# The values' raw compression weights loaded with the second key block into a pool of their own, their last block after the prompt's attention scratch, and the prompt mLSTM denominators on VectorE alone

## The chip, the cores and the metric

The kernel runs on one core of a Trainium2 chip. Its time is the device time of one execution in microseconds (us). Engines are named as in the profile: PE is TensorE (PEld its weight load, PEq its sequencer), DVE VectorE, ACT ScalarE, POOL GpSimd, SP SyncE, which here does nothing but issue DMAs.

## What is computed

The reference is one decoder layer of a hybrid model: a prompt of 512 tokens and a decode step for eight sample rows go through attention over paged caches (compressed blocks, selected blocks and a window) beside an mLSTM, then a projection, cross attention and an MLP. Two pieces of it matter here. The first compresses cached keys and values: 16 rows of the cache make a chunk, and two neighbouring chunks go through a two-layer perceptron.

```
def compress(kv, pe, w1, b1, w2):
    ch = kv.reshape(b, nc, CMP_STRIDE, hk, dh).transpose(0, 1, 3, 2, 4).reshape(b, nc, hk, half)
    first = ch @ w1[:half]
    second = ch @ w1[half:]
    second = jnp.concatenate([second[:, 1:], jnp.zeros_like(second[:, :1])], axis=1)
    hid = first + second + (pe.reshape(-1) @ w1 + b1)
    return jax.nn.gelu(hid) @ w2
k_cmp = compress(kc_all, *w['cmp_k'])
v_cmp = compress(vc_all, *w['cmp_v'])
```

`w1` has 2048 x 256 entries, 2 MB for the keys and 2 MB for the values. The second piece is the denominator of the mLSTM:

```
den = jnp.sum(a, axis=2) + w_inter * jnp.einsum('bhd,blhd->blh', n, qi)
h_out = num / jnp.maximum(jnp.abs(den), jnp.exp(-m_q))[..., None]
```

## The kernel before, in words

The stage runs from about 235 to 440 us. It is written as Python generators that are woven together: in the background `compress(0)` (keys) and then `compress(1)` (values), in the foreground a chain of `front()` (the prompt's mLSTM, with the prompt's attention over compressed blocks, `cmp_prompt`, in between), `mlstm_s` (the mLSTM of the sample rows) and `sample` (their attention). A scheduler then sets each engine's order; every engine takes its own instructions strictly in that order, and pools of buffers decide what may be in flight. Engines that are ready have no way past an instruction that waits.

`compress` walks over 8 blocks b of cached rows and 4 parts t of the 2048 rows of `w1`. For each t, `load_w1` (L583 to L588) fetches the raw weights by four DMAs of 128 KB, and `weights` splits them: a high half `w1h` by ScalarE (L213), the low half `w1l` = raw minus high by VectorE (L214), and GpSimd adds two raw halves to `ws` (L1134). TensorE then multiplies three times (L218 high x high, L219 low x high, L220 high x low) and once with the sum (L1296). `xf`, `xh`, `xl`, `xs` are the gathered rows, turned and split in the same manner; `cgat` is where gathers (POOL, L573) put them.

The raw weights of the values lie in three places. `wr` holds t = 0 and 1 (eight DMAs, 1 MB). `vcn` holds t = 2. `po` (`po2` in the code) and `r` (`r3`) hold the halves of t = 3. The key weights went through `vcn`, `po` and `r` too, so these are used twice. In the kernel before, `wr` is a tile of the pool `w1r`, which is opened, together with `pp` (the prompt columns of the values, L1167 and L1168), only when the prompt's mLSTM is done; all four parts are loaded there, with the two `vcn` halves as their previous readers allow and `po` as early as its last key reader permits.

`cmp_prompt` handles four tiles i of 128 prompt tokens. Each has a scratch `csb` (128 x 256): scores plus mask by VectorE (L1369), minimum (L1371, L1372), difference by POOL (L1373), exponential by ScalarE, sum and reciprocal on VectorE (L1376 to L1378), gates (L1379), product by POOL (L1380); TensorE transposes it (L1387) and ScalarE puts it into `PcT` (L1388). `csb` has two buffers in a pool. `cmp_consts` uses one of them earlier as `cd`.

The prompt's mLSTM projects with `wqk` (L781, one buffer, loaded for the next head after the present one's last use, L802) by L799 and L802, and closes each tile with `dn`: an absolute value by ScalarE (L835), maximum (L836) and reciprocal (L837) by VectorE, and a scaling by ScalarE (L838). `mlstm_s` follows with L948 to L1120: transpositions L991, scores L1006 and `As` (L1009 to L1012), `n0T` (L1035 on TensorE, L1036 on VectorE), state transpositions L1058 into `CT`, and L1065, the product with the old state, which needs them. `nxt<-cur` (L1305, L1306) are small DMAs of the compression.

Of the kernel before, what the change touches and what calls it, by code (L numbers as in the profile page):

```python
# [6 lines left out]
F32 = mybir.dt.float32  # L7
# [4 lines left out]
OP = mybir.AluOpType  # L12
# [24 lines left out]
def body(tc, I, O, stage=99, dbg=None):  # L37
    nc = tc.nc
    with ExitStack() as top:
# [37 lines left out]
        def push(name, **kw):  # L77
            st = ExitStack()
            right[name] = st
            return pool(name, stack=st, **kw)  # L80

        def pop(name):
            right.pop(name).close()
# [682 lines left out]
        def mlstm():  # L766
# [62 lines left out]
            def value(h, i):  # L829
# [4 lines left out]
                dn = ml.tile([128, 1], F32, name="dn", bufs=4)  # L834
                nc.scalar.activation(dn, pn[:, 128:129], AF.Abs)  # L835
                nc.vector.tensor_tensor(dn, dn, eN[:, i, h:h + 1], op=OP.max)  # L836
                nc.vector.reciprocal(dn, dn)  # L837
# [98 lines left out]
        def cmp_consts(pk_):  # L936
            CB = pk_.tile([128, 4, 8, 32], F32, name="CB")
            cd = pk_.tile([128, 8, 32], F32, name="csb", bufs=2)[:, 0:4]
            nc.gpsimd.iota(cd, pattern=[[128, 4], [-16, 32]], base=-31, channel_multiplier=1,
# [181 lines left out]
        def compress(kv):  # L1121
# [49 lines left out]
            def produce(b, t):  # L1171
# [9 lines left out]
                if b == 0 and t > 0:  # L1181
                    weights(t, raws[t])
                if kv == 0 and b > 0 and "w" not in cgs and "ml" not in right and "mlstm" in done:
                    wp_ = push("w1r", side="left")
                    cgs["w"] = wp_.tile([128, 2, 2, 2, 256], F32, name="wr")
                    prompt_cols(1, r3, wp_.tile([128, 512], F32, name="pp"))
                    for u in range(4):
                        load_w1(1, u, [cgs["w"][:, u, s] for s in range(2)] if u < 2 else
                                ([vr[:, s] for s in range(2)], pr_)[u - 2])
                xf = cw.tile([128, 4, 128], F32, name="xf", bufs=2)  # L1190
# [14 lines left out]
                if b == 0 and t == 3:  # L1205
                    if kv == 1:
                        pop("w1r")
                    done.add(("w", kv))
# [136 lines left out]
        def cmp_prompt():  # L1345
# [17 lines left out]
            for i in range(5):  # L1363
                if i < 4:
                    sb = pk_.tile([128, 8, 32], F32, name="csb", bufs=2)
                    S = bank(psp)
# [467 lines left out]
        def front():  # L1834
            cb = cgs["cb"] = cmp_prompt()
            n = 0
            for x in mlstm():
                yield x
                n += 1
                if ("p", 0) in done and n % 2 == 0:  # L1840
                    next(cb, None)

        fg = chain(paced(front(), 1.3), paced(mlstm_s(), 2), paced(sample(), .8), open_late())
        flip[1] = 4
# [772 lines left out]
```

## Time and profile before

| | us |
|---|---|
| median of 3 runs | 1234.26 |
| lowest and highest of the 3 | 1231.63, 1235.07 |
| the profiled execution's own time | 1243.24 |
| its span (first to last instruction) | 1241.5 |
| TensorE busy in the span | 1174.3 (95%) |
| VectorE, ScalarE, GpSimd busy | 841.2, 612.4, 558.6 |
| mean granted TensorE clock | 0.974 |

Rows of the profile give a start and a duration in us, the engine, the line, output and input by the names of the program, and in brackets how long the engine had been idle and what ended that. Busy times of windows and the granted clock (1.00 is 2.4 GHz, 0.50 is 1.2 GHz) are read side by side: an engine that is nearly always busy in a window bounds it, and TensorE that is busy at half clock is slow without being idle.

### The profile page before, as it was taken

Reading aid. Unit: us, or ns where it says so; the run is one execution under the profiler, and the core shown is the slowest. Engines: PE = TensorE matmul, PEld = TensorE weight load, DVE = VectorE, ACT = ScalarE, POOL = GpSimd, SP = SyncE. Lnnn points to the kernel's source line nnn. Section 1 sums busy time; section 2 is a strip of 40 time slices with the busy share of each in tenths; the row PEclk is TensorE's granted clock in tenths of the full one; section 3 lists DMA queues with packets and bytes.
Section 4 is the critical chain, followed back from the end, with each engine's and each line's share of the span. In section 5 each row is a group of like instructions: output and inputs, shape, how many; then the busy total and the mean of one; then the engine's idle time right before and its main releaser. Section 6 shows DMA issues by size and latency. Waiting matters only on the chain.

```text
span 1241.5 us, 24581 instructions
## 1 busy us (share of the span) xinstructions
PE 1174.3 (95%) x9220; PEld 1066.7 (86%) x9220; DVE 841.2 (68%) x1901; ACT 612.4 (49%) x1414; POOL 558.6 (45%) x686
## 2 busy tenths in 40 slices
PE   7999999899997989988999989999899999999996
PEld 5998999588885878854999987599899999999996
DVE  6337683567787687653754756554998888888874
ACT  5235665745545444466542423342665565555452
POOL 1013353566666266542342100043885576476342
PEclk9999999899997999999999998999999999999998
DMA  7324240141253185566767298630032333322411
GB/s 232 102 53 105 86 153 1 51 137 44 78 171 115 42 283 176 178 227 205 206 135 171 83 239 288 231 128 2 1 119 86 103 96 107 106 94 77 137 52 73
DMA packets 141769, 154.30 MB, mean 124 GB/s; under 512 B 17449, under 2 KB 123689, under 8 KB 141394
## 3 DMA queue, kind: packets, MB, share of 16 engines
q1 hardware_dynamic: 131922, 119.17, 32.0%
q0 software_dynamic: 9728, 33.56, 8.3%
q8 instruction: 73, 1.20, 0.4%
q14 instruction: 46, 0.38, 0.1%
HBM read 141.67 MB, written 13.12 MB: 125 GB/s over the span
## 4 chain that ended last, share of the span: by engine, by line
PE 49%; DVE 8%; ACT 3%; DMA 2%; issue 2%; SPq 1%; POOL 1%; POOLq 0%; DVEq 0%; ACTq 0%
PE xc L2291 7%; PE xa L2291 7%; PE bd L2291 5%; PE tp L2291 5%; PE bd L220 3%; PE bd L219 3%; PE bd L218 3%; DVE sp L2231 1%; DMA mkv<-in_cache_mem_k 1%; PE xa L1296 1%; PE tp L1518 1%; PE bd L2190 1%; PE xa L218 1%; PE xa L219 1%; PE xa L220 1%
## 5 line engine op out<-in xcount | busy, mean ns | idle before, releaser
L214 POOL TENSOR_TENSOR al<-fraw,ah 128x512 fp32r<-128x512 f32 (+1 forms) x104 | 127.5, 1227 | 152.4 <-ACT ah L213 124.0
L213 ACT ACTIVATE whi<-wraw 128x1024 fp32r<-128x1024 f32 (+3 forms) x74 | 62.5, 890 | 57.5 <-DMA wraw<-in_w_xv 28.2
L214 DVE TENSOR_TENSOR wlo<-wraw,whi 128x1024 fp32r<-128x1024 f32 (+3 forms) x74 | 73.6, 1026 | 19.1 <-ACT whi L213 19.0
L213 ACT ACTIVATE ah<-fraw 128x512 fp32r<-128x512 f32 (+1 forms) x112 | 65.8, 593 | 38.0 <-PE xc L2291 11.8
L218 PE MATMUL bd<-w1h,xh 128*128 128x256 f32 x256 | 82.6, 325 | 0.9 <-issue 0.9
L220 PE MATMUL bd<-w1h,xl 128*128 128x256 f32 x256 | 75.6, 298 | 3.0 <-DVE xl L214 3.0
L1198 POOL TENSOR_TENSOR xs<-xf 128x256 f32<-128x256 f32 x64 | 55.8, 878 | 50.2 <-PE xa L1296 30.5
L219 PE MATMUL bd<-w1l,xh 128*128 128x256 f32 x256 | 75.7, 297 | 0.0
L1296 PE MATMUL xa<-ws,xs 128*128 128x256 f32 x256 | 71.2, 400 | 2.4 <-DVE bq L1470 1.3
L625 POOL TENSOR_SCALAR sb<-sb,rs,gat 128x128 f32<-128x128 f32 (+3 forms) x64 | 46.1, 724 | 54.4 <-DVE rs L624 40.2
L213 ACT ACTIVATE xh<-xf 128x512 fp32r<-128x512 f32 x64 | 40.0, 629 | 45.5 <-DVE xf L1191 20.0
L213 ACT ACTIVATE ah<-sp 128x512 fp32r<-128x512 f32 (+1 forms) x64 | 35.5, 555 | 50.1 <-DVE sp L2231 22.8
L220 PEld LDWEIGHTS bd<-w1h,xl 128*128 128x128 f32 x256 | 48.9, 192 | 6.4 <-DVE xl L214 3.8
L1296 PEld LDWEIGHTS xa<-ws,xs 128*128 128x128 f32 x256 | 46.5, 201 | 8.5 <-issue 2.9
L218 PEld LDWEIGHTS bd<-w1h,xh 128*128 128x128 f32 x256 | 49.1, 193 | 5.0 <-issue 3.9
L214 DVE TENSOR_TENSOR xl<-xf,xh 128x512 fp32r<-128x512 f32 x64 | 47.5, 746 | 8.6 <-ACT xh L213 7.7
L219 PEld LDWEIGHTS bd<-w1l,xh 128*128 128x128 f32 x256 | 49.4, 193 | 4.5 <-issue 2.8
L219 PE MATMUL bd<-hlo,whi 128*128 128x272 f32 x176 | 52.0, 296 | 0.0
L218 PE MATMUL bd<-hhi,whi 128*128 128x272 f32 x176 | 51.7, 294 | 0.0
L1191 DVE STREAM_TRANSPOSE xf<-cgat 128x512 f32<-128x512 f32 x64 | 44.7, 703 | 10.2 <-POOL xs L1198 8.4
L220 PE MATMUL bd<-hhi,wlo 128*128 128x272 f32 x176 | 51.3, 292 | 0.0
L2231 DVE TENSOR_TENSOR sp<-fraw 128x512 f32<-128x512 f32 (+1 forms) x32 | 47.8, 1494 | 0.2
(990 smaller groups left out, 4667.9 us busy)
## 6 DMA issues: line engine op xcount, KB each, us to landing
fraw<-in_w_gate SPq DMA_DIRECT2D x11, 1024.0 KB
fraw<-in_w_up SPq DMA_DIRECT2D x11, 1024.0 KB
fraw<-in_w_down SPq DMA_DIRECT2D x24, 384.0 KB
mkv<-in_cache_mem_k SPq DMA_DIRECT2D x64, 128.0 KB
mkv<-in_cache_mem_v SPq DMA_DIRECT2D x16, 512.0 KB
wraw<-in_w_in SPq DMA_DIRECT2D x8, 512.0 KB
wraw<-in_w_xq SPq DMA_DIRECT2D x4, 1024.0 KB
wraw<-in_w_xk SPq DMA_DIRECT2D x4, 1024.0 KB
```

The source lines that it names most:

```text
L213: nc.scalar.activation(hi, src, AF.Copy)
L214: (eng or nc.gpsimd).tensor_tensor(lo, src, hi, op=OP.subtract)
L218: nc.tensor.matmul(out, ah, bh, start=first, stop=False, **kw)
L219: nc.tensor.matmul(out, ah, bl, start=False, stop=False, **kw)
L220: nc.tensor.matmul(out, al, bh, start=False, stop=last, **kw)
L625: (nc.vector, nc.gpsimd)[1].tensor_scalar(sb[:, :n], sb[:, :n], rs, gat[:, i, 3 * h + 1 + br:3 * h + 2 + br], op0=OP.mult, op1=OP.mult)
L1191: nc.vector.transpose(xf.rearrange("p a (q i) -> p q a i", q=4), gs[0].rearrange("p (q t a i) -> p t q a i", q=4, t=4, a=4)[:, t])
L1198: nc.gpsimd.tensor_tensor(xs_.rearrange("p c (v j) -> p v c j", v=2), xg[:, 0], xg[:, 1], op=OP.add)
L1296: nc.tensor.matmul(dst[2], ops[2][:, kk], w1s[t][2][:, kk], start=t == 0 and kk == 0, stop=t == 3 and kk == 1, skip_group_check=True)
L1518: nc.tensor.transpose(p[:, 128 * i:128 * i + 128], srcs(i), ident)
L2231: nc.vector.tensor_tensor(o, a, b, op=op)
L2291: nc.tensor.matmul(p[:, :HALF], w[a][:, k], x[b_][:, k], start=first and k == 0 and i == 0, stop=last and k == n - 1 and i == 2, skip_grou ...
```

## The change

Three edits go together. First, the pool `w1r` with the tile `wr` is opened before the foreground chain is made, and the weights of the values for t = 0 and 1 are loaded when block b = 1 of the keys is produced, one part with t = 0 and one with t = 1; after the mLSTM a second pool `w1p` holds only `pp`, and only t = 2 and 3 are loaded there. Second, to make room, the scratch of `cmp_prompt` is no longer a tile of its own: `csb` uses the two halves of `po2` by turns, and `cd` uses the first of them. Third, the denominators: VectorE computes max(-den, e) straight from PSUM, then the maximum with den, so that ScalarE's absolute is gone.

```diff
--- before.py
+++ after.py
@@ -832,8 +832,9 @@
                     nc.tensor.matmul(pn[:, :129], st["A", h, k][:, 128 * (i - k):128 * (i - k) + 128], vmn[:, k, h],
                                      start=k == 0, stop=k == i)
                 dn = ml.tile([128, 1], F32, name="dn", bufs=4)
-                nc.scalar.activation(dn, pn[:, 128:129], AF.Abs)
-                nc.vector.tensor_tensor(dn, dn, eN[:, i, h:h + 1], op=OP.max)
+                e = eN[:, i, h:h + 1]
+                nc.vector.scalar_tensor_tensor(dn, pn[:, 128:129], -1.0, e, op0=OP.mult, op1=OP.max)
+                nc.vector.tensor_tensor(dn, dn, pn[:, 128:129], op=OP.max)
                 nc.vector.reciprocal(dn, dn)
                 nc.scalar.activation(hN[:, h, i], pn[:, :128], AF.Copy, scale=dn)
                 jk = ml.tile([128, 128], B16, name="jk")
@@ -935,7 +936,7 @@
 
         def cmp_consts(pk_):
             CB = pk_.tile([128, 4, 8, 32], F32, name="CB")
-            cd = pk_.tile([128, 8, 32], F32, name="csb", bufs=2)[:, 0:4]
+            cd = po2[:, 0:128].rearrange("p (i s) -> p i s", i=4)
             nc.gpsimd.iota(cd, pattern=[[128, 4], [-16, 32]], base=-31, channel_multiplier=1,
                            allow_small_or_imprecise_dtypes=True)
             for h in range(8):
@@ -1180,13 +1181,14 @@
                         gather_cmp(*nxt, q)
                 if b == 0 and t > 0:
                     weights(t, raws[t])
+                if kv == 0 and b == 1 and t < 2:
+                    load_w1(1, t, [cgs["wv"][:, t, s] for s in range(2)])
                 if kv == 0 and b > 0 and "w" not in cgs and "ml" not in right and "mlstm" in done:
-                    wp_ = push("w1r", side="left")
-                    cgs["w"] = wp_.tile([128, 2, 2, 2, 256], F32, name="wr")
+                    wp_ = push("w1p", side="left")
+                    cgs["w"] = cgs.pop("wv")
                     prompt_cols(1, r3, wp_.tile([128, 512], F32, name="pp"))
-                    for u in range(4):
-                        load_w1(1, u, [cgs["w"][:, u, s] for s in range(2)] if u < 2 else
-                                ([vr[:, s] for s in range(2)], pr_)[u - 2])
+                    for u in (2, 3):
+                        load_w1(1, u, ([vr[:, s] for s in range(2)], pr_)[u - 2])
                 xf = cw.tile([128, 4, 128], F32, name="xf", bufs=2)
                 nc.vector.transpose(xf.rearrange("p a (q i) -> p q a i", q=4),
                                     gs[0].rearrange("p (q t a i) -> p t q a i", q=4, t=4, a=4)[:, t])
@@ -1204,6 +1206,7 @@
                     st["e", t] = hi, lo
                 if b == 0 and t == 3:
                     if kv == 1:
+                        pop("w1p")
                         pop("w1r")
                     done.add(("w", kv))
                 st[b, t] = [(xh[:, :, g], xl[:, :, g]) for g in range(2)] + [xs_]
@@ -1362,7 +1365,7 @@
             yield
             for i in range(5):
                 if i < 4:
-                    sb = pk_.tile([128, 8, 32], F32, name="csb", bufs=2)
+                    sb = po2[:, 256 * (i % 2):256 * (i % 2) + 256].rearrange("p (h s) -> p h s", h=8)
                     S = bank(psp)
                     for v in range(2):
                         nc.tensor.transpose(S[:, 128 * v:128 * v + 128], ST[:, v, 128 * i:128 * i + 128], ident)
@@ -1840,6 +1843,7 @@
                 if ("p", 0) in done and n % 2 == 0:
                     next(cb, None)
 
+        cgs["wv"] = push("w1r", side="left").tile([128, 2, 2, 2, 256], F32, name="wr")
         fg = chain(paced(front(), 1.3), paced(mlstm_s(), 2), paced(sample(), .8), open_late())
         flip[1] = 4
         burst(fg, 8)
```

SyncE's order near the middle of `compress(0)`, after the prompt columns `xf<-cd` of the keys. `wqk` are the projection weights of head 2, `po_3201` and `r_3207` the buffers of t = 3. Before:

```order
L1156 DMA hidt<-in_cmp_pe_k 4x256
L1157 DMA hidt<-in_cmp_b_k 4x32
L1167 DMA xf<-cd_81 128x1x512
L588 DMA po_3201<-in_cmp_w_v 128x1x256 x2
L1167 DMA r_3207<-cd_82 128x1x512
L781 DMA wqk<-in_w_qm 128x128
L781 DMA wqk<-in_w_km 128x128
L756 DMA out<-kcT 24x512
L757 DMA out<-kcT 3x512
L1305 DMA nxt<-cur 112x256
```

After:

```order
L1157 DMA hidt<-in_cmp_pe_k 4x256
L1158 DMA hidt<-in_cmp_b_k 4x32
L1168 DMA xf<-cd_81 128x1x512
L588 DMA wr<-in_cmp_w_v 128x1x256 x8
L781 DMA wqk<-in_w_qm 128x128
L781 DMA wqk<-in_w_km 128x128
L1168 DMA r_3207<-cd_82 128x1x512
L756 DMA out<-kcT 24x512
L757 DMA out<-kcT 3x512
L1308 DMA nxt<-cur 112x256
```

The eight `wr` loads have come in ahead of `wqk`, the two `po` loads have gone, and the prompt columns into `r` stand behind `wqk`.

SyncE's order where the mLSTM of the prompt ends. Before:

```order
L954 DMA n_4539<-in_state_n 32x128
L956 DMA n_4541<-in_state_n 8x512
L1305 DMA nxt<-cur 112x256
L1306 DMA nxt<-cur 15x256
L1305 DMA nxt<-cur 112x256
L1306 DMA nxt<-cur 15x256
L588 DMA wr<-in_cmp_w_v 128x1x256 x8
L588 DMA r_3207<-in_cmp_w_v 128x1x256 x2
L1091 DMA out<-nsn 8x512
L1156 DMA hidt<-in_cmp_pe_v 4x256
```

After:

```order
L955 DMA n_4546<-in_state_n 32x128
L957 DMA n_4548<-in_state_n 8x512
L588 DMA po_3201<-in_cmp_w_v 128x1x256
L1308 DMA nxt<-cur 112x256
L1309 DMA nxt<-cur 15x256
L588 DMA po_3201<-in_cmp_w_v 128x1x256
L588 DMA r_3207<-in_cmp_w_v 128x1x256 x2
L1150 DMA w_5307<-in_cmp_w_v 128x2x64
L1157 DMA hidt<-in_cmp_pe_v 4x256
```

Ten loads of the values' weights before, four after, and two of these (`po`) are loads that stood at the early place.

VectorE's order right behind `wc`, a small vector of the samples' mLSTM (about 369 us in the trace before). `w1l_...` are the low halves of the values' weights. Before:

```order
L973 TENSOR_TENSOR wc<-m_99,smS 4x8
L214 TENSOR_TENSOR xl<-xf,xh 128x2x4x64
L1332 TENSOR_TENSOR ys<-xa,cur 128x256
L1234 SCALAR_TENSOR_TENSOR hid<-hidt,hid 128x512
L1372 TENSOR_SCALAR cmn<-cmn 128x8
L962 TENSOR_SCALAR nsl<-sel 4x128
L982 COPY msk<-bm 32x32
L1000 COPY bm_4623<-bm 32x8 x3
L1191 STREAM_TRANSPOSE xf<-cgat 128x4x4x32
L214 TENSOR_TENSOR xl<-xf,xh 128x2x4x64
L1333 TENSOR_TENSOR ys<-ys,bd 128x256
```

After:

```order
L974 TENSOR_TENSOR wc<-m_99,smS 4x8
L1336 TENSOR_TENSOR ys<-ys,bd 128x256
L1337 TENSOR_TENSOR ys<-bd,nxt 128x256
L214 TENSOR_TENSOR w1l_5302<-wr,w1h_5301 128x1024
L214 TENSOR_TENSOR xl<-xf,xh 128x2x4x64
L963 TENSOR_SCALAR nsl<-sel 4x128
L214 TENSOR_TENSOR xl<-xf,xh 128x2x4x64
L1375 TENSOR_SCALAR cmn<-cmn 128x8
L214 TENSOR_TENSOR w1l_5340<-wr,w1h_5339 128x1024
L208 COPY kcT<-xc 128x127
L1193 STREAM_TRANSPOSE xf<-cgat 128x4x4x32
L214 TENSOR_TENSOR w1l_5361<-vcn,w1h_5360 128x1024
```

Three splits of the values' weights stand here now; before, that of `vcn` stood 26 rows behind `wc` and the two of `wr` some 20 rows behind that.

## Rows read from the trace of the kernel before

**Rows 1.** The head of the page: span, and each engine's busy time, share and instructions.

```profile
span 1241.5 us, 24581 instructions
PE 1174.3 (95%) x9220; PEld 1066.7 (86%) x9220; DVE 841.2 (68%) x1901; ACT 612.4 (49%) x1414; POOL 558.6 (45%) x686
```

**Rows 2.** Windows of the stage: start and end, length, then busy us (and instructions) of PE, PEld, DVE, ACT and POOL, the granted clock, the share of the DMA engines that is busy, and GB/s.

```profile
262.00:360.00 98.00, 96.86 (x700) 85.30 (x699) 70.59 (x170) 50.79 (x149) 63.51 (x76) 1.00 0.28 85
360.00:378.00 18.00, 16.02 (x108) 13.93 (x107) 15.03 (x41) 7.35 (x18) 12.03 (x19) 0.91 0.65 194
378.00:392.00 14.00, 8.38 (x66) 6.16 (x64) 12.87 (x24) 9.94 (x20) 12.76 (x12) 0.72 0.42 130
392.00:412.00 20.00, 17.32 (x101) 14.32 (x101) 11.16 (x22) 10.57 (x26) 5.41 (x7) 0.68 0.15 51
```

**Rows 3.** The timeline of TensorE in the hole: start, duration, engine, line, operation.

```profile
381.04 0.44 PE L1387 MATMUL tp<-ident,csb 128*128 128x128 f32 x2
...
383.70 0.44 PE L1006 MATMUL tp<-qsT,ksT 128*32 128x32 f32 x8 [1.79 <-ACT PcT L1388]
...
387.68 1.91 PE L1016 MATMUL tp<-wi,sel 4*128 4x32 f32 x8 [2.94 <-DVE As L1012]
...
391.44 0.58 PE L218 MATMUL bd<-w1h,xh 128*128 128x256 f32 x1 [0.85 <-issue]
...
398.14 0.24 PE L1035 MATMUL tp<-ident,n 32*128 32x32 f32 x1
...
402.62 1.11 PE L1216 MATMUL xc<-ident,ys 128*128 128x128 f32 x4 [2.67 <-ACT kcT L206]
...
408.90 0.43 PE L1065 MATMUL po<-CT,Qz 128*32 128x129 f32 x8
```

**Rows 4.** The timeline of ScalarE: the splits that waited for a raw weight.

```profile
390.33 1.06 ACT L213 ACTIVATE w1h<-wr 128x1024 fp32r<-128x1024 f32 x1 [2.98 <-DMA wr<-in_cmp_w_v]
...
399.29 1.06 ACT L213 ACTIVATE w1h<-wr 128x1024 fp32r<-128x1024 f32 x1 [3.23 <-DMA wr<-in_cmp_w_v]
401.76 0.63 ACT L213 ACTIVATE w1h<-r 128x512 fp32r<-128x512 f32 x1 [1.42 <-DMA r<-in_cmp_w_v]
```

**Rows 5.** The timeline of VectorE: the low halves of weights, of a key weight (246.25) and of the values' weights, and `n0T`.

```profile
246.25 1.21 DVE L214 TENSOR_TENSOR w1l<-vcn,w1h 128x1024 fp32r<-128x1024 f32 x1
...
379.26 2.83 DVE L214 TENSOR_TENSOR w1l<-vcn,w1h 128x1024 fp32r<-128x1024 f32 x1
...
391.42 2.07 DVE L214 TENSOR_TENSOR w1l<-wr,w1h 128x1024 fp32r<-128x1024 f32 x1 [0.54 <-issue]
...
400.38 1.33 DVE L214 TENSOR_TENSOR w1l<-wr,w1h 128x1024 fp32r<-128x1024 f32 x1 [6.13 <-ACT w1h L213]
402.43 1.21 DVE L214 TENSOR_TENSOR w1l<-r,w1h 128x512 fp32r<-128x512 f32 x1 [0.71 <-ACT w1h L213]
403.56 0.18 DVE L1036 COPY n0T<-tp 128x32 f32<-128x32 f32 x1
```

**Rows 6.** The timeline of SyncE: when a DMA, or a run of equal ones, was issued, and how long the issuing took with its waits in between.

```profile
245.07 0.54 SPq L1167 DMA_DIRECT2D xf<-cd  x1
248.13 1.12 SPq L588 DMA_DIRECT2D po<-in_cmp_w_v  x2
251.27 0.52 SPq L1167 DMA_DIRECT2D r<-cd  x1
251.89 0.41 SPq L781 DMA_DIRECT2D wqk<-in_w_qm  x1
...
381.06 7.02 SPq L588 DMA_DIRECT2D wr<-in_cmp_w_v  x8
388.18 5.90 SPq L588 DMA_DIRECT2D r<-in_cmp_w_v  x2
```

**Rows 7.** Windows of the two half-clock stretches in the hole, columns as in group 2.

```profile
401.30:408.10 6.80, 5.49 (x23) 4.83 (x24) 5.46 (x11) 3.60 (x8) 2.41 (x2) 0.50 0.01 3
384.20:397.90 13.70, 9.90 (x47) 7.83 (x48) 9.42 (x21) 8.80 (x23) 7.20 (x8) 0.50 0.46 146
```

**Rows 8.** DMA traffic of SyncE's queue: packets, MB and the share of the 16 engines' time, first from 216 to 230 us (key weights, no gathers), then from 247 to 252.2 and from 388 to 394 (both beside gathers).

```profile
q1 hardware_dynamic: 1081, 0.92, 19.9%
...
q1 hardware_dynamic: 286, 0.39, 21.1%
...
q1 hardware_dynamic: 320, 0.32, 18.4%
```

**Rows 9.** The timeline of POOL beside the 2.83 us split.

```profile
379.68 1.27 POOL L1134 TENSOR_TENSOR ws<-vcn 128x512 f32<-128x512 f32 x1
380.93 1.74 POOL L1198 TENSOR_TENSOR xs<-xf 128x256 f32<-128x256 f32 x1
```

**Rows 10.** The tile `dn`: least, median and greatest duration in ns, first and last start; below, the idle time of L838's engine before it, with its count.

```profile
L835 ACT ACTIVATE dn<-tp x16: 149/160/179, 258.1 to 321.7; 128x1 f32<-128x1 f32 x16
L836 DVE TENSOR_TENSOR dn<-dn,eN x16: 118/151/768, 259.4 to 322.4; 128x1 f32<-128x1 f32 x16
...
  DVE dn L837: 14.0, 9
```

**Rows 11.** The timeline of TensorE: the last use of the `wqk` of head 1, and the first of head 2.

```profile
251.36 0.30 PE L802 MATMUL tp<-xc,wqk 128*128 128x32 f32 x2
...
262.30 1.02 PE L799 MATMUL tp<-xc,wqk 128*128 128x512 f32 x2
```

## The prediction

> **What bounds the kernel now.** I read the head of the page first: TensorE is busy 1174.3 of 1241.5 us, VectorE 841.2 [rows 1]. An average of 95% leaves little to win anywhere except in a hole, so the second view is the table of windows around the stage that the change touches. From 262 to 360 us TensorE works 96.86 of 98 us at full clock; from 360 to 378 the others close up (VectorE 15.03 of 18); from 378 to 392 TensorE works only 8.38 of 14 while VectorE works 12.87; from 392 to 412 TensorE is busy 17.32 of 20, but at a mean granted clock of 0.68 [rows 2]. So the hole lies between 378.5 and 412, and it has two halves with different limits. In the first, VectorE is the queue that everybody waits for. In the second it is the raw weights: TensorE's idle rows in the hole are 1.79, 2.94, 0.85 and 2.67 us (8.25 in all), the last one ended by `kcT` on ScalarE [rows 3], and ScalarE itself stood before that behind three weight splits, 2.98 and 3.23 us for `wr` and 1.42 for `r` [rows 4]. VectorE shows the same from its side: 6.13 and 0.71 us idle before the two low-half splits `w1l<-wr` and `w1l<-r`, and only after them `n0T`, whose transpose on TensorE (L1035, 398.14) had run five us earlier [rows 3, 5]. Those loads could not land sooner, since SyncE issues the eight `wr` loads from 381.06 on and the two `r` loads from 388.18 [rows 6].
>
> The hole costs clock too. Two stretches in it run at half clock (granted 0.50, that is 1.2 GHz): TensorE was busy 9.90 us in the first and 5.49 in the second [rows 7]. At full clock these would be half as long, so the hole's price beside its 8.25 us of idleness is up to (9.90 + 5.49) / 2 = 7.7 us.
>
> **The change, part by part.**
>
> *Eight of the late loads become early ones.* Of the `wr x8`, `po x2` and `r x2` loads of the value weights, `po` was early before, `wr` is early now, and `po` is late now. Late are four loads (0.5 MB) in place of ten (1.3 MB). What goes: VectorE's 6.13 + 0.71 = 6.84 us of idle time [rows 5]. I take that as the term, since VectorE is the engine whose rows stand behind it and which `n0T` and `CT` need. TensorE's own 2.67 + 0.85 us would be the low reading, the whole 8.25 the high one.
>
> *What is late next.* The `po` buffer is now the scratch of the prompt attention (`csb`), so its value weights can come only when the last transposition of that scratch, L1387 at 381.04 [rows 3], has read it. With that step later by up to three splits that now stand ahead of it (3 x 1.21 to 3 x 2.83 = 3.6 to 8.5 us [rows 5]), it runs at 385 to 390. Half a megabyte at the rate of such loads (0.92 MB in the 14 us from 216 to 230, of which they filled 10 to 11, so about 90 GB/s; 0.32 MB in 6 us, 53 GB/s, beside the gathers [rows 8]) takes 6 to 10 us. The last raw weight is then there at 391 to 400, where before its split began at 401.76 [rows 4]. So the wait shrinks by 2 to 11 us, and 6.84 lies in the middle of that.
>
> *The clock.* With the second half of the hole gone, its half-clock stretch (401.3 to 408.1) goes as well: 5.49 / 2 = -2.7 us. The first stretch I leave, since it follows VectorE's busy half, which the change does not shorten.
>
> *The splits move.* Both `w1l<-wr` and `w1l<-vcn` now stand right behind `wc` on VectorE, around 369 us, in the part where the GpSimd sums and gathers run. Alone such a split took 1.21 us; beside GpSimd's `ws` and `xs` sums it took 2.83; the two of `wr` took 2.07 and 1.33 before [rows 5, 9]. Bounds: at 1.21 each they give back 0.98 us; at 2.83 each they cost 5.66 - 3.40 = +2.26. I take +2.26, because there is no quiet place for them in a stretch where VectorE has only 3 of 18 us free [rows 2] and each brings its own `ws` sum with it.
>
> A rule of the Trainium skill bears on this ("SBUF — State Buffer", section "SBUF: two separate sides"): a VectorE operation with two inputs in SBUF and a GpSimd operation that reads SBUF share one pair of ports as an exclusive lock, so the later one waits out the other in full. It speaks against the change, which moves two-input splits into GpSimd's busy stretch. The rows agree with it as far as they go: 2.83 us is more than 1.21 plus the 1.27 of the `ws` sum beside it [rows 5, 9]. By the rule each moved split would wait out its own `ws` sum at least, 1.21 + 1.27 = 2.48 us, a term of 4.96 - 3.40 = +1.6 and a sum of -8.0; without it the term would be -0.98 and the sum -10.5.
>
> *Denominators.* Sixteen ScalarE absolutes (0.160 us median) go, 2.6 us in all. Sixteen VectorE operations come on top of the sixteen that were there (0.151 median) [rows 10]: 2.4 us more, perhaps 0.3 us each where one reads PSUM beside waiting queues. This lies from 258 to 322 us, where TensorE works 96.86 of 98 us [rows 2], and it hides them. ScalarE waited 14.0 us there for the reciprocals, at no cost to TensorE. One handing-over (ScalarE to VectorE) falls away and one dependent VectorE operation comes. Value taken 0, bounds -1 and +2.4.
>
> *Early queue.* The eight `wr` loads now stand on SyncE between `xf<-cd` (245.07) and the projection weights `wqk` of head 2 [rows 6]. Their buffer is new and free, so they start between 245.6 (when `xf<-cd` is issued) and 248.1 (where the two `po` loads stood). Ahead of `wqk` stand 1.05 MB. The gathers nearby fill some 5 us at 0.39 MB in 5.2 us (75 GB/s), the rest goes at 90 [rows 8]: 12 to 13 us, with `wqk` itself (0.13 MB) 1.5 more. Landed at 259 to 262. TensorE wants it for L799 at 262.30 [rows 11]. Value taken 0; the wait that replaces it is a rival below.
>
> *The reordering.* The mLSTM sample chain (L991 to L1065) now stands some 50 matmuls further back. Those are compression matmuls of 0.12 us that ran inside the hole before and now run ahead of it: the same work, so no term, but they no longer fill the hole, which bounds the gain from above.
>
> Sum: -6.84 - 2.7 + 2.26 + 0 + 0 = **-7.3 us**. The profiled execution has a span of 1241.5 and a time of 1243.24 us; the median of the three runs is 1234.26 (1231.63 to 1235.07), so the profiled one is 9 us slower than the median, and I carry the difference over: 1234.26 - 7.3 = 1227. About 0.3% (3.7 us) is what a measurement of this kernel can tell from no change.
>
> **The rivals.**
>
> *A, the forecast*, 1227. Its own range: at best -6.84 - 2.7 - 0.98 = -10.5 (1223.7), at worst the splits and VectorE's extra 2.4 us in full and no clock back, -6.84 + 2.26 + 2.4 = -2.2 (1232). For it: the order behind `w1l<-r` is a queue that stood still with work ready (`n0T`).
>
> *B, the hole only moves*, 1231 to 1237. VectorE is already busy 15.03 of 18 us and 12.87 of 14 [rows 2]. The splits put into that stretch delay the scratch chain, hence the late `po` and `r` loads, hence the same `w1l<-r` in the same queue; the wait at 400 becomes a wait at 390 that is reached with less compression work in hand. Then only the 2.67 us of TensorE come back or nothing does: -2.7 to +2.4. For it: a chain that had some 11 us of VectorE rows between its mask and its weights gets three splits in between. Against: the raw weights were the last to come, by the rows.
>
> *C, slower: head 2 waits for its weights.* The eight loads reach `wqk`'s queue first. If they ran at the 53 GB/s seen beside gathers all the way, 1.18 MB take 22.3 us, from 245.6 to 248.1: landed at 268 to 270.4, so TensorE, in order, stands 5.6 to 8.1 us at L799, then works at half clock. A stall of 8.25 us cost up to 7.7 in clock in the hole, and 2.7 at least, so the price is up to 10.8 to 15.8, less the 7.3 won: +3.5 to +8.5, that is 1238 to 1243, say 1240. It decides from a landing at about 267, where it eats the gain. Against: the loads at 216 to 230 ran at twice that rate, and gathers fill 10 us of these 22 at most.
>
> *D, the larger gain*, 1218 to 1222. VectorE's 3 free us before 378 take the splits for nothing, its queue in 378 to 391 is shorter by `w1l<-vcn` (2.83), and the idle rows 1.79 and 2.94 go with the first half-clock stretch: 8.25 + 7.7 = -16 at most, from -12.
>
> **How the numbers follow.** A 0.50, B 0.26, C 0.11, D 0.13. A is 1223.7 to 1232; a seventh of it lies within 0.3% of 1234.26 (1230.6 to 1238.0), 0.07. B is nearly all there: 0.20 within, 0.02 faster, 0.04 slower counting a chain that comes out later than the waits give back. C is slower for 0.10, within for 0.01. So faster 0.43 + 0.02 + 0.13 = 0.58, same 0.28, slower 0.14. The range takes A, B but its last us, and half of D: 1219 to 1238. Left out are C and the low half of D, about 0.17.
>
> **What would show it.** In the changed profile: eight `wr` loads near 246 to 253; `w1l<-wr` without a DMA in its idle column; the first L1065 near 400 rather than 408.90; no half clock behind it; idle before `w1l<-r` below 2 us. L799 of head 2 with no idle above 1 us (else C). Splits near 369 of about 2.8 us (else D, if 1.2). I am wrong if TensorE's idle time between 360 and 412 stays near 10 us with VectorE as the releaser (B).

## The result

The change made the kernel slower. In the first comparison it took 1243.79 us (median of 10 runs, 1241.23 to 1249.39) against 1238.18 (10 runs, 1231.63 to 1242.84): a ratio of 1.006, interval 1.0037 to 1.0082. Measured once more beside other kernels it was 1.0017 (0.9996 to 1.0039; 12 and 35 runs), so the loss is some 2 to 7 us, and the second interval just reaches no loss at all. The forecast was 1227. The profiled execution of the changed kernel took 1245.99 us.

The page's head, to be read against [rows 1], shows hardly any difference in work, but one in span:

```profile
span 1244.2 us, 24591 instructions
PE 1174.0 (94%) x9220; PEld 1065.2 (86%) x9220; DVE 836.8 (67%) x1917; ACT 612.1 (49%) x1398; POOL 561.0 (45%) x686
```

The windows of the stage, same columns as [rows 2]:

```profile
262.00:360.00 98.00, 91.97 (x644) 80.34 (x642) 66.51 (x163) 46.62 (x130) 55.41 (x70) 0.97 0.25 75
360.00:378.00 18.00, 18.00 (x133) 16.64 (x132) 17.48 (x38) 8.63 (x18) 13.46 (x15) 1.00 0.53 159
378.00:392.00 14.00, 9.00 (x71) 7.87 (x69) 12.66 (x20) 6.36 (x14) 13.89 (x14) 1.00 0.66 194
392.00:412.00 20.00, 15.83 (x109) 12.34 (x109) 17.92 (x49) 11.31 (x28) 13.66 (x16) 0.78 0.32 101
412.00:440.00 28.00, 28.00 (x229) 23.11 (x227) 17.71 (x56) 16.57 (x50) 5.86 (x8) 0.91 0.09 26
266.00:274.00 8.00, 6.04 (x21) 4.77 (x22) 0.97 (x3) 1.63 (x4) 0.00 (x0) 0.57 0.14 51
```

The stretch from 262 to 360, which TensorE filled before, has lost 4.9 us of its work (96.86 to 91.97), and the last row shows where: at 266 to 274 TensorE runs at a granted clock of 0.57, near its lower level. The hole is still there, though it looks otherwise: 378 to 392 has as little TensorE work as before (9.00 us, but at full clock), and VectorE, which had 6 idle us in one piece around 397, is now busy 17.92 of 20 us from 392 to 412.

TensorE's timeline at both places, with the idle time and its releaser in brackets:

```profile
267.96 2.05 PE L799 MATMUL tp<-xc,wqk 128*128 128x512 f32 x2 [4.75 <-DMA wqk<-in_w_qm]
...
273.97 1.02 PE L825 MATMUL sp<-qm,kmT 128*128 128x512 f32 x2
...
393.29 0.18 PE L1028 MATMUL sp<-ident,wT 4*32 4x4 f32 x1 [5.68 <-DVE As L1010]
...
404.17 0.44 PE L1390 MATMUL tp<-ident,po 128*128 128x128 f32 x2
...
417.74 0.65 PE L1066 MATMUL po<-CT,Qz 128*32 128x129 f32 x16
```

Head 2's first projection began at 262.30 before [rows 11] and now at 267.96, after a wait of 4.75 us for its weights. The first score product behind it (L825) comes at 273.97, 8.4 us after its place in the trace before:

```profile
265.58 1.02 PE L825 MATMUL sp<-qm,kmT 128*128 128x512 f32 x2
```

Of this, 5.7 us are waiting and starting late, the rest half clock. This is the prediction's rival C. In the hole the last scratch is transposed at 404.17 (before 381.04 [rows 3]), the first product with the old state comes at 417.74 (before 408.90 [rows 3]), and the last update of the new state at 443.5 (before 438.5), as the last starts of these lines say, before and after:

```profile
L1099 DVE SCALAR_TENSOR_TENSOR C<-C,wcb,tp x32: 330/344/351, 422.9 to 438.5; 128x128 f32<-128x128 f32 x32
L1100 DVE SCALAR_TENSOR_TENSOR C<-C,wcb,tp x32: 306/342/349, 427.5 to 443.5; 128x128 f32<-128x128 f32 x32
```

So of 8.4 us lost at the projection the hole gave back 3.4 by then, and some 5 us stay. That is of the size of the measured loss; the two executions shown end only 2.7 us apart, so one pair of traces does not size it closer.

SyncE's timeline shows why the projection waited; compare [rows 6]:

```profile
244.17 0.54 SPq L1168 DMA_DIRECT2D xf<-cd  x1
244.81 12.24 SPq L588 DMA_DIRECT2D wr<-in_cmp_w_v  x8
257.15 1.22 SPq L781 DMA_DIRECT2D wqk<-in_w_qm  x1
```

Issuing the eight loads took 12.24 us (single ones between 0.53 and 4.12 us; the profile names nothing that SyncE waited for, so why is not shown), and `wqk` was issued at 257.15 instead of 251.89. DMA traffic from 249 to 256 us, first the gathers (q0), then SyncE's queue (q1), as packets, MB and share of the engines' time:

```profile
q0 software_dynamic: 317, 1.04, 48.8%
q1 hardware_dynamic: 331, 0.33, 16.5%
```

Beside the gathers SyncE's queue moved 0.33 MB in 7 us, 47 GB/s, below the lowest rate that I had read (53 [rows 8]), and gathers ran for some 16 of the 18 us from 249 to 267, not for five. By the packets of the trace the eight loads ran from 248.3 to 267.1 us, and those of `wqk` ended at 267.5.

### The profile page after: what moved, and what is told of

Read it like the earlier page. It is cut to its first block, busy times and chain, and to the rows that moved or that the text cites. A ratio compares the mean times of both kernels' runs of the same rounds, so it can differ in the third digit from the quotient of the medians.

```text
span 1244.2 us, 24591 instructions
## 1 busy us (share of the span) xinstructions
PE 1174.0 (94%) x9220; PEld 1065.2 (86%) x9220; DVE 836.8 (67%) x1917; ACT 612.1 (49%) x1398; POOL 561.0 (45%) x686
## 4 chain that ended last, share of the span: by engine, by line
PE 73%; DVE 9%; DMA 6%; ACT 4%; issue 3%; POOL 2%; SPq 1%; POOLq 0%; DVEq 0%; ACTq 0%
PE xc L2295 7%; PE xa L2295 7%; PE bd L220 7%; PE bd L218 7%; PE bd L219 7%; PE bd L2295 5%; PE tp L2295 5%; PE xa L1299 3%; PE xc L219 1%; PE xc L218 1%; PE xc L220 1%; PE tp L634 1%; DMA wraw<-in_w_xv 1%; PE xa L218 1%; PE xa L219 1%
## 5 line engine op out<-in xcount | busy, mean ns | idle before, releaser
L214 DVE TENSOR_TENSOR wlo<-wraw,whi 128x1024 fp32r<-128x1024 f32 (+3 forms) x74 | 73.5, 1023 | 24.0 <-ACT whi L213 23.9
L1200 POOL TENSOR_TENSOR xs<-xf 128x256 f32<-128x256 f32 x64 | 51.2, 806 | 61.6 <-PE xa L1299 34.3
L214 DVE TENSOR_TENSOR xl<-xf,xh 128x512 fp32r<-128x512 f32 x64 | 51.4, 808 | 8.1 <-ACT xh L213 5.0
L1909 POOL TENSOR_TENSOR acc<-acc,sq 128x272 f32<-128x272 f32 x35 | 30.7, 876 | 36.8 <-ACT sq L1908 36.5
```

The lines of the kernel that those rows point to most:

```text
L214: (eng or nc.gpsimd).tensor_tensor(lo, src, hi, op=OP.subtract)
L1200: nc.gpsimd.tensor_tensor(xs_.rearrange("p c (v j) -> p v c j", v=2), xg[:, 0], xg[:, 1], op=OP.add)
L1909: nc.gpsimd.tensor_tensor(acc[hf], acc[hf], sq, op=OP.add)
```

## The experiments

Five theories stand behind them. 1: the loss is TensorE's wait at head 2 for `wqk`. 2: it is in the hole, where splits and sums stand ahead of the last scratch chain. 3: the denominators cost by themselves. 4: the selection stage (540 to 600 us) falls to half clock by chance or by order. 5, formed after the first eight runs: GpSimd's sums ahead of `bm` keep the hole open. All times are ratios to the kernel before, run on the same chip, with 95% intervals.

### gated: the early loads behind the last `wqk`

```diff
                 evac(dst, p, scl)
+                if (h, w) == (3, 0):
+                    nc.vector.tensor_copy(cgs["wr"][0:1, :, :, :, 0:1].rearrange("p t s c o -> p (t s c) o"),
+                                          dst[0:1, 0:1, None].to_broadcast([1, 8, 1]))
...
-                if kv == 0 and b == 1 and t < 2:
+                if kv == 0 and b == 4 and t < 2:
```

> This is the changed kernel with one thing moved: the eight loads into wr wait until the q projection of the last head is out (a one-row copy from it into wr, on VectorE, stands before them), so that no wqk load has them ahead; all else, the late part of VectorE's order too, is as in the changed kernel. Theory 1 (the loss is TensorE's wait for the wqk of head 2, with the half clock behind it, about 8 us at 274 us): no idle over 1 us at head 2's first L799, TensorE busy 36 or more of 38 us from 262 to 300, the first product with the old state 7 to 9 us earlier than 417.7, and a time 6 to 8 us under the changed kernel's, 0.997 to 1.001 of the kernel before. Theory 2 (the loss is in the hole, where three splits and three GpSimd sums stand ahead of the last scratch chain): the stall goes, but the time stays within 2 us of the changed kernel's, 1.004 or more of the kernel before.

Measured 1.0029 (1.0008 to 1.0051). The wait at head 2 is gone, and TensorE is busy 37.70 of 38 us from 262 to 300:

```profile
263.11 1.02 PE L799 MATMUL tp<-xc,wqk 128*128 128x512 f32 x2
...
388.83 0.18 PE L1031 MATMUL sp<-ident,wT 4*32 4x4 f32 x1 [5.68 <-DVE As L1013]
```

The first product with the old state came at 413.3, 4.4 us earlier than in the changed kernel, not 7 to 9. The 5.68 us of idleness in the hole stand as they were. And the wait at head 2 was not only taken away but in part moved: the held-back loads now stand on SyncE ahead of the small DMA `nxt<-cur`, VectorE waits for that, and TensorE for VectorE. SyncE's, VectorE's and TensorE's rows:

```profile
282.85 7.24 SPq L588 DMA_DIRECT2D wr<-in_cmp_w_v  x8
290.19 1.32 SPq L1311 DMA_DIRECT2D nxt<-cur  x1
...
300.99 0.42 DVE L1340 TENSOR_TENSOR ys<-bd,nxt 128x256 f32<-128x256 f32 x1 [5.95 <-DMA nxt<-cur]
...
302.50 0.39 PE L220 MATMUL bd<-w1h,xl 128*128 128x256 f32 x1 [2.81 <-DVE xl L214]
```

So gated is not the changed kernel without its loss, and its time does not decide between theories 1 and 2.

### dn_only, twice: the denominators alone

```diff
-                nc.scalar.activation(dn, pn[:, 128:129], AF.Abs)
-                nc.vector.tensor_tensor(dn, dn, eN[:, i, h:h + 1], op=OP.max)
+                e = eN[:, i, h:h + 1]
+                nc.vector.scalar_tensor_tensor(dn, pn[:, 128:129], -1.0, e, op0=OP.mult, op1=OP.max)
+                nc.vector.tensor_tensor(dn, dn, pn[:, 128:129], op=OP.max)
```

> The kernel before with the denominators on VectorE alone, nothing else. Theory 1 and 2: 0.998 to 1.002 of the kernel before, since TensorE is busy 97% there; the 14 us of ScalarE's waiting become shorter or longer at no cost. Theory 3 (one more dependent VectorE step of each tile stands in VectorE's queue behind larger rows and delays the mLSTM's end): 2 to 6 us slower, the last scaling of the mLSTM (322.8 us before) 2 us or more later.

> The kernel before with the denominators on VectorE alone, once more: its first time was 0.8% over the kernel before, while its profile was 1.5 us ahead at 440 us and lost 7 us between 440 and 602, with 24 us at half clock there against 7. Theory 4 (half clock in the selection stage falls differently in each execution): 1.000 to 1.005 this time, other half-clock stretches in 540 to 600. If the order of this kernel makes it: 1.005 to 1.011 and the same stretches at 542, 572 and 586.

Measured 1.008 (1.0048 to 1.0111), then 1.0057 (1.0027 to 1.0086). A surprise, and not by the way that theory 3 says: the tile's rows in the first run are

```profile
L836 DVE SCALAR_TENSOR_TENSOR dn<-tp,eN x16: 120/148/159, 258.6 to 322.2; 128x1 f32<-128x1 f32 x16
L837 DVE TENSOR_TENSOR dn<-dn,tp x16: 104/152/156, 260.5 to 322.4; 128x1 f32<-128x1 f32 x16
...
  DVE dn L838: 14.1, 10
```

against [rows 10]: the operations last 0.15 us each, ScalarE waits 14.1 us for the reciprocals as it did (14.0), and the mLSTM's last scaling starts at 322.8, as before (at 325.4 in the second run). What differs is behind that. The edit changed the scheduler's order far past its own lines, and from 440 to 600 us (selection and compression of the values) TensorE got less done at a lower clock, here the kernel before, then the first and the second run of this one:

```profile
440.00:600.00 160.00, 143.51 (x1260) 112.12 (x1259) 102.22 (x272) 84.79 (x174) 80.45 (x98) 0.98 0.67 215
```

```profile
440.00:600.00 160.00, 142.57 (x1209) 109.49 (x1208) 98.56 (x263) 81.64 (x167) 80.73 (x96) 0.93 0.64 204
```

```profile
440.00:600.00 160.00, 142.82 (x1218) 110.31 (x1217) 98.32 (x269) 82.59 (x167) 78.87 (x95) 0.95 0.65 207
```

By the clock's own rows in the traces that is 23.9 and 17.1 us at the lower level against 6.8. Both executions have it, at about the same four places (near 450, 545, 575 and 590 us), so it goes with the order and is not theory 4's chance. How much of the loss it makes is not shown: csb_only, below, has 17.1 us at the lower level in the same stretch and is 2.3 us slower, and the two profiled executions here span 1242.0 and 1240.5 us, about as much as the one of the kernel before (1241.5), though the medians of their kernels are higher.

### csb_only: the scratch in `po` alone

```diff
-            cd = pk_.tile([128, 8, 32], F32, name="csb", bufs=2)[:, 0:4]
+            cd = po2[:, 0:128].rearrange("p (i s) -> p i s", i=4)
...
-                    sb = pk_.tile([128, 8, 32], F32, name="csb", bufs=2)
+                    sb = po2[:, 256 * (i % 2):256 * (i % 2) + 256].rearrange("p (h s) -> p h s", h=8)
```

> The kernel before with the prompt attention's scratch (csb, cd) in po, nothing else; the ten loads of the values' weights are all late, po now among them: twelve. Theory 1: the hole ends on the r load, which now comes behind po, so 1 to 3 us slower, 1.001 to 1.003. Theory 2: the late po and r are what undid the gain in the hole: 4 us or more slower, 1.003 or more.

Measured 1.0019 (1.0000 to 1.0037), 2.3 us: theory 1's size, though the interval reaches into theory 2's. The late `po` blocks cost little here.

### gated_mix: half of the scratch in `po`, one buffer of its own

```diff
-                    sb = po2[:, 256 * (i % 2):256 * (i % 2) + 256].rearrange("p (h s) -> p h s", h=8)
+                    sb = (pk_.tile([128, 8, 32], F32, name="csb", bufs=1) if i % 2 else
+                          po2[:, 0:256].rearrange("p (h s) -> p h s", h=8))
```

> As gated, but the scratch uses the first half of po and one buffer of its own by turns, so that of the last three late loads one po block can come early and the other does not wait for the last scratch. Theory 1: as gated within 2 us. Theory 2 (late po and r hold the hole open): 2 to 5 us faster than gated, the last low-half split of r (410 or later in the changed kernel) 4 us or more earlier.

Measured 1.011 (1.008 to 1.014), against both theories. TensorE's wait behind `nxt<-cur` is there as in gated (3.16 us), its wait for `As` too (5.69 us), and behind that a second stretch at half clock from 402 to 416 us; the low half of `r` starts at 408.92, only 2.4 us earlier than in gated. So the wait for `As` does not hang on the late loads. Why this order is so much worse I did not settle.

### after_again, no_dn, gated_nodn

The changed kernel again, and the changed kernel and gated with ScalarE's absolute back.

> The changed kernel once more, for a second profile and a time beside the others of this call: 1.004 to 1.008 of the kernel before. Theory 1 (head 2's wait for wqk): again idle of 4 to 5 us at its first L799. Theory 4 (in the selection stage, 540 to 600 us, TensorE has few rows to work on and its clock is near falling; which order the change leaves there decides how long it runs at half clock): half clock there for 15 us or more again, against 4 before. If that was chance: under 8.

> The changed kernel with ScalarE's absolute back. Theory 1: the same wait for wqk, so 1.003 to 1.007 of the kernel before. Theory 3 (the denominators cost by themselves, as the run with them alone was 0.8% slower): 4 to 9 us faster than the changed kernel, 0.998 to 1.002 of the kernel before.

> The changed kernel with the wr loads held back behind the last wqk and ScalarE's absolute back. Theory 1 and 3 together: the two losses both go, what is left is the hole's gain, 2 to 5 us faster than the kernel before (0.996 to 0.998). If the hole only moved: 0.999 to 1.002.

Measured 1.0017 (0.9996 to 1.0039), 1.0022 (1.0002 to 1.0041) and 1.0049 (1.0025 to 1.0073). The second profile of the changed kernel repeats the wait at head 2 (4.90 us, 4.75 before) and the 5.68 us for `As`; its half clock from 540 to 600 is 13.7 us after 17.1, between the two expectations. Without the new denominators the wait at head 2 stays, at 5.90 us, and nothing is gained: theory 3 falls, the denominators have no price that could be added to others. The run also bears on theory 5, since in it `bm` comes early, `msk` is short and the 5.68 us for `As` are not there:

```profile
377.48 0.16 DVE L982 COPY msk<-bm 32x32 f32<-32x32 f32 x1
```

The last update of the state came at 440.1 then (443.5 in the changed kernel), and the time is the same all the same: the wait for `As` can go without a gain. Held back and without the new denominators (gated_nodn), the kernel has no wait at head 2 and yet is the slowest of the three. Here the moved wait of gated is larger, with half clock behind it from 301.9 to 308.7:

```profile
304.34 0.42 DVE L1339 TENSOR_TENSOR ys<-bd,nxt 128x256 f32<-128x256 f32 x1 [8.10 <-DMA nxt<-cur]
...
305.08 2.07 PE L828 MATMUL sp<-qm,kmT 128*128 128x512 f32 x2 [5.41 <-DVE A L830]
```

### wr_rows: the same megabyte in narrower loads

```diff
-                    load_w1(1, t, [cgs["wv"][:, t, s] for s in range(2)])
+                    w1 = I["cmp_w1_v"][0].rearrange("(s r t c j) o -> t s r j c o", s=2, r=4, t=4, c=2)
+                    for s in range(2):
+                        for r in range(4):
+                            nc.sync.dma_start(cgs["wv"][32 * r:32 * r + 32, t, s], w1[t, s, r])
```

> The changed kernel with the early megabyte in 16 loads of 32 rows (64 KB) in place of eight of 128 rows, the same bytes at the same place ahead of wqk. If the loads were slow because each of the eight ran on few DMA engines and shared them with the gathers: the megabyte lands in 8 us or less, the wait at head 2's first L799 is under 2 us, and the time falls by 4 to 8 us against the changed kernel. If the bytes ahead of wqk count and not how they are spread: the wait stays at 3 us or more.

Measured 0.9987 (0.9972 to 1.0002), some 4 us under the changed kernel measured beside it (1240.31 and 1244.26). SyncE's rows, TensorE's, and the traffic from 249 to 256 us, the stretch shown for the changed kernel, here SyncE's queue first:

```profile
244.91 7.39 SPq L1188 DMA_DIRECT2D wr<-in_cmp_w_v  x11
252.40 0.37 SPq L781 DMA_DIRECT2D wqk<-in_w_qm  x1
```

```profile
265.61 1.02 PE L799 MATMUL tp<-xc,wqk 128*128 128x512 f32 x2
```

```profile
q1 hardware_dynamic: 1093, 0.80, 42.8%
q0 software_dynamic: 299, 0.96, 42.8%
```

Beside 0.96 MB of gathers (1.04 in the changed kernel) SyncE's queue moved 0.80 MB in these 7 us, `wqk` among them, 114 GB/s where the wide loads had 47, and its share of the 16 engines' time went from 16.5% to 42.8%. The packets in the traces say the same: of the wide loads four were under way at a time for most of the stretch and seldom more than five, of the narrow ones up to 16, and the last of the megabyte ended at 257.6, not at 267.1. That is 11.6 us from its first packet at 246.0, not the 8 expected, against 18.8. So the wide loads were too narrowly spread.

There is no wait at L799. (It comes at 265.61 and not at 262.30 all the same; csb_only, which has no early load, has it at 265.40.) One thing was not as meant: the scheduler put five of the sixteen loads behind `wqk`, so 0.7 MB stood ahead of it and not 1.05. In the changed kernel the first 0.7 MB were through at 260.1, and with its 0.13 MB at 47 GB/s `wqk` would have been there at about 263, an estimate, which is early enough for 265.61 too. So that the wait is gone does not tell the spread from the number of bytes ahead; the rates and the end of the whole megabyte do. At the last update of the state this kernel is 4.6 to 5.4 us ahead of the two traces of the changed one (438.1; 442.7 and 443.5), so its gain lies ahead of the selection stage.

### rows_hold and rows_hold_nodn: the splits behind the scratch

wr_rows, and in `cmp_prompt` behind the last `PcT`:

```diff
+                    if i == 4:
+                        x_ = cgs["wv"][0:1, :, :, 0, 0:1].rearrange("p t s o -> p (t s) o")
+                        nc.vector.scalar_tensor_tensor(x_, PcT[0:1, 0, 511:512, None].to_broadcast([1, 4, 1]), 0.0, x_,
+                                                       op0=OP.mult, op1=OP.add)
```

> The early megabyte in 16 loads of 32 rows, and the splits and sums of wr held until the last scratch is transposed (a four-element operation on VectorE that adds nought times an element of PcT to wr). Theory 5 (in the changed kernel the hole keeps 5.7 us of TensorE's idleness because GpSimd's sums of the early weights stand ahead of bm, on which VectorE's msk waits, then As): msk takes under 0.5 us, TensorE's wait for As falls below 1 us, and the last scratch is transposed 8 us or more earlier than in the run with rows alone (398.9). The time is 2 to 6 us under that run's, 0.994 to 0.997 of the kernel before. If VectorE's amount of work sets the hole's length and not the place of the sums: the waits move to another row, and the time stays within 2 us of the run with rows alone.

> The same with ScalarE's absolute back in the denominators. If the denominators cost nothing, as TensorE is busy 97% beside them: within 2 us of the run before it in this call. If they cost 5 us or more by themselves: 4 us or more faster than that run.

First the rows of the changed kernel that these two answer, VectorE and then GpSimd:

```profile
388.27 0.20 DVE L1010 TENSOR_SCALAR As<-sp,uNs 32x32 f32<-32x32 f32 x1
389.00 3.18 DVE L983 COPY msk<-bm 32x32 f32<-32x32 f32 x1 [0.53 <-POOL bm L980]
...
392.68 0.55 DVE L1010 TENSOR_SCALAR As<-sp,uNs 32x32 f32<-32x32 f32 x3
```

```profile
382.68 3.07 POOL L1135 TENSOR_TENSOR ws<-wr 128x512 f32<-128x512 f32 x1
385.70 1.17 POOL L978 TENSOR_SCALAR_AFFINE_SELECT bm<-bm 32x8 f32<-32x8 f32 x1
...
387.57 1.25 POOL L1135 TENSOR_TENSOR ws<-wr 128x512 f32<-128x512 f32 x1
388.79 0.18 POOL L980 TENSOR_SCALAR_AFFINE_SELECT bm<-bm 32x8 f32<-32x8 f32 x1
388.96 1.25 POOL L1135 TENSOR_TENSOR ws<-vcn 128x512 f32<-128x512 f32 x1
390.18 0.60 POOL L1376 TENSOR_TENSOR po<-po,cmn 128x256 f32<-128x256 f32 x1
390.75 1.40 POOL L1200 TENSOR_TENSOR xs<-xf 128x256 f32<-128x256 f32 x2
```

`bm`, a small mask, stands on GpSimd behind two sums of the early weights (3.07 and 1.25 us). VectorE's copy `msk` waits for it, and then lasts 3.18 us, until the four GpSimd operations behind `bm` are done (the last three rows); three of the four `As` stand behind that, and TensorE behind `As`: 5.68 us. With the splits held, the rows of VectorE and TensorE in rows_hold, and of VectorE in rows_hold_nodn, are

```profile
380.04 0.63 DVE L983 COPY msk<-bm 32x32 f32<-32x32 f32 x1
```

```profile
385.10 0.18 PE L1028 MATMUL sp<-ident,wT 4*32 4x4 f32 x1 [3.26 <-DVE As L1010]
...
389.89 1.12 PE L1250 MATMUL xc<-hid,w 128*64 128x127 f32 x8 [2.77 <-DVE hid L1240]
...
393.79 0.69 PE L1393 MATMUL tp<-ident,po 128*128 128x128 f32 x2 [1.30 <-POOL po L1386]
```

```profile
373.07 0.16 DVE L982 COPY msk<-bm 32x32 f32<-32x32 f32 x1
```

rows_hold measured 1.0016 (0.9990 to 1.0041): `msk` is short again, the last scratch comes 5.1 us earlier (393.79 against 398.91 in wr_rows) rather than 8, and the waits moved to other rows of VectorE, which was the rival expectation. With no_dn that makes two runs in which the wait that theory 5 names is gone or shorter and no time is gained. rows_hold_nodn measured 0.9978 (0.9960 to 0.9996), 6.5 us under rows_hold measured beside it, and is the one version clearly faster than the kernel before: 1236.13 against 1239.10. In it the last scratch reached `PcT` at 386.1 (395.0 in rows_hold), TensorE was busy 45.58 of 52 us from 360 to 412 (41.25 in rows_hold, 41.72 before), and the last update of the state came at 435.3 (438.5 before). What the denominators add is thus the order again: without them `wc` stands at 371.24, nearer to the kernel before (368.51) than in rows_hold (374.34), and the scratch chain with it.

## Why the prediction was wrong

Two steps failed, and rivals B and C came true together.

**The step that turned a gain into a loss is the one called "Early queue"**, where 0 was taken. Its rival C, given 0.11, is what happened: `wqk` landed at 267.5, where C said 268 to 270.4, and TensorE stood 4.75 us. What was mis-sized is the rate. The loads started about where the step had them, at the late end (their packets run from 248.3, behind the 256 KB of `xf<-cd`), but I counted gathers for "some 5 us" and 75 GB/s beside them and 90 for the rest; gathers ran for 16 of 18 us, with 47 GB/s beside the first batch, and the 1.18 MB took 19.2 us, 62 GB/s. The row for the second batch was in the trace before: GpSimd issues gathers from 257.83 on, too. I also left out the time to issue eight loads (12.24 us here, 7.02 in the trace before [rows 6]), but `wqk` was issued at 257.15 and landed ten us later, so it was the loads still running that it waited for. The price of the rival was put too high (10.8 to 15.8): by the next score product 8.4 us were lost.

**Late loads become early ones: right for the loads, wrong for the time.** ScalarE splits `wr` at 375.03 and 378.48 without waiting, and VectorE has no idle time above 1 us from 380 to 411. But the term of -6.84 needed nothing else to be late at that place, and it is the second step that failed: wr_rows, which has no wait at head 2, gained not 7.3 us but some 1.6 (0.9987). That is rival B, given 0.26, with its own sign: TensorE's idle time from 360 to 412 stayed at 9.2 us (10.3 before), its longest piece released by VectorE. The prediction named the late `po` and `r` as next; csb_only puts them at 2.3 us, and the changed kernel's longest wait in the hole is not for them. What came was a wait that I had not looked for: GpSimd's order. I had placed the splits on VectorE and forgotten that the sums which they bring stand in front of `bm` and the scratch's subtractions on GpSimd. What that wait is worth is not shown: without it the idle time stood at other rows (rows_hold), or the time was the same (no_dn).

**What is late next** put the last scratch at 385 to 390. It came at 404.17, or 396 when the 8.4 us of head 2 are taken off; 6 to 11 us late.

**The splits move: +2.26 was too much, and on the wrong engine.** The moved splits took 1.20, 1.20 and 1.48 us, almost undisturbed; for the two of `wr` that is 2.40 against 3.40, the lower bound of -0.98:

```profile
380.32 1.20 DVE L214 TENSOR_TENSOR w1l<-wr,w1h 128x1024 fp32r<-128x1024 f32 x1
...
383.39 1.20 DVE L214 TENSOR_TENSOR w1l<-wr,w1h 128x1024 fp32r<-128x1024 f32 x1
...
385.35 1.48 DVE L214 TENSOR_TENSOR w1l<-vcn,w1h 128x1024 fp32r<-128x1024 f32 x1
```

It was the sum `ws` (1.27 us alone) that took 3.07, and `msk`. By the rule of the Trainium skill ("SBUF — State Buffer", section "SBUF: two separate sides") whichever of the two engines starts first with an operation that needs the shared ports holds them for that instruction, and the other waits, GpSimd as well as VectorE. The trace agrees for the splits: beside them GpSimd's rows are the long ones and VectorE's are not. (By the profile `ws` began at 382.68 and the VectorE operation beside it at 382.72, but starts on GpSimd are rough.) For `msk` it shows more than the rule says: that copy waited out four GpSimd instructions and not one. I had applied the rule to one side only.

**The clock: the wrong stretch.** The stretch that was to go (401.3 to 408.1 [rows 7]) is still there, as long as before, at 410.0 to 416.8. What shrank is the part that the prediction left as it was: 3.4 us from 370.6 and 13.7 from 384.2 became 6.8 from 392.9. So half clock from 300 to 440 fell from 23.9 us to 13.7; at half work per us that is 5 us, near the 2.7 of the prediction in size by luck only, and part of the 3.4 us that the hole gave back. Another 6.8 us of half clock came behind head 2's wait.

**Denominators: right in every row, and wrong as a term.** Durations and waits came out as said. That an edit which costs nothing on the chip changes a scheduler's order elsewhere, for up to 0.8%, was not in the sum. Of the changed kernel this explains nothing that was measured, since it was no faster without them (1.0022 and 1.0017), while rows_hold was 6.5 us faster without them; the effect is not additive.

**Shown and not shown.** Shown: the wait at head 2, that it is gone in wr_rows, with some 4 us gained, and that loads of 32 rows move faster beside gathers; that the same loads held back make a like wait at the next small DMA; the sums ahead of `bm`, and that holding the splits shortens `msk`. Not shown: that the wait behind `bm` costs time, and how much of dn_only's loss is half clock. Open: why the order of gated_mix is so slow, and why half clock falls where it does from 540 to 600 us; the changed kernel's two executions differ there by 3.4 us.

## What to carry to other kernels

A load that is moved earlier is paid for by the small load behind it: look at who stands next in the same queue, wherever the load is moved to, and at the rate that loads of this shape have in a stretch like the one where they will run, gathers included. When an input comes early, every engine's part of the work comes early, so follow each of the parts into its own queue. And under a scheduler an edit that is free on the chip still reorders the rest: compare the order far behind the edit before calling it nothing.

## What the runs showed of the hardware

A copy of 32x32 elements on VectorE, 0.16 us alone, took 3.18 us while GpSimd ran four operations one after another beside it (388.96 to 392.15): it ended only with the last of them.

In the same seven us (249 to 256) and beside about as many gathers (1.04 and 0.96 MB) SyncE's queue moved 47 GB/s of loads of 128 rows and 114 GB/s with loads of 32 rows. The wide loads had four packets under way at a time for most of the stretch, beside gathers and without them (the key weights, 216 to 231 us in the trace before); the narrow ones had up to 16. The whole megabyte took 18.8 us in the one shape and 11.6 in the other.
